# The two ends of a one-core decoder step: first transfers on two queues, products of zeros ahead of the first real ones, and a last tile added in halves

## The chip, the core and the metric

The kernel runs on one core of one Trainium2 chip. The metric is the device time of one execution in microseconds. Three runs of the kernel before took 982.81, 983.32 and 984.39 us; 983.32 is their median. The trace and the page of the profile come from one further execution, which took 982.86 us, with a span of 981.1 us from its first instruction to its last.

The engines are named as the profile names them: PE is TensorE's products and PEld its weight loads, DVE is VectorE, ACT is ScalarE, POOL is GpSimd, SP is SyncE, which issues transfers (SPq is its queue of instructions).

## What is computed

One layer of a hybrid decoder on 512 prompt positions and 8 x 4 new tokens, 544 rows of 2048 numbers in all, in float32:

```python
def rms_norm(x, g):
    xf = x.astype(jnp.float32)
    y = xf * lax.rsqrt(jnp.mean(xf * xf, axis=-1, keepdims=True) + EPS)
    return (y * g.astype(jnp.float32)).astype(x.dtype)

def project(x, g, w_in):
    z = jnp.einsum('bsd,de->bse', rms_norm(x, g), w_in)   # 2048 -> 6144: q, k, v, ga, u, gp
    ...

def merge(x, attn_o, ga, pool_o, gp, w_out):
    mix = jnp.concatenate([attn_o.reshape(b, s, ATTN_WIDTH) * jax.nn.silu(ga),
                           pool_o * jax.nn.silu(gp)], axis=-1)
    return x + jnp.einsum('bse,ed->bsd', mix, w_out)
...
y_prompt = rms_norm(hp, final_norm_g)
y_sample = rms_norm(hs, final_norm_g)
```

Between the two projections stand a windowed attention (16 heads, three dilations), for the new tokens against a cache of 2048 positions, and a pooling over 2 to 16 positions. The caches are also written out again, shifted by the new tokens. Only the input projection's first products and the last norm matter here.

## The kernel before

**Three products for one.** Every float32 operand of a large product is split into a high part, rounded to the fast float32r form, and the low rest: ScalarE makes the high part (`xH`, `wH`), VectorE subtracts it from the whole and keeps the rest (`xL`, `wL`). TensorE then adds up xH·wH, xL·wH and xH·wL in a PSUM bank.

**Order.** All instructions are written out by hand, engine by engine; nothing reorders them afterwards. A model of the engines' times inside the program (`Clock`, `Paced`) decides while the program is written out at which place of TensorE's stream the attention's pieces go. Each engine works through its list in order, and stands still where an operand isn't there. All transfers are issued by SP, in order; an issue waits where the eighth transfer before it hasn't landed, or where its buffer is in use.

**The first stage.** x comes in transposed, as 16 tiles of 128 x 544 (`x_load(d)`, 272 KB each). The first two blocks of 128 output columns (a q and a k block) are made together, tile by tile of x: for each d there are 12 products of 272 columns (two blocks, three parts, two halves of the 544 rows). Their weights come in tiles of 128 x 1024; tiles 0 and 2 are loaded and split in halves (`w_part`, `w_split`). For each d the loop calls `x_split(d)`: ScalarE makes xH (times the norm's gain, a column of the constants `c[:, C_G:]`) and the square of x, VectorE makes xL; VectorE also adds up the squares (`x_sum`). The norm's factor is applied to the finished block.

`PA` is a tile of zeros that GpSimd clears at the start; `qms` are two operands of the attention that are set to zero from it.

**The tail.** The output projection runs over four blocks of 512 columns. In each, 16 tiles e of the inner dimension are multiplied into five accumulators, four of 128 prompt rows (t = 0 to 3) and one of the new tokens (t = 4). In the last block the products of e = 10 to 15 are put off, so that the tiles finish one after the other: for each t there are 18 products of 512 columns, then an add of the input rows (`add_rows`, VectorE), the sum of squares (`squares_of`, ScalarE), the norm (`norm_of`: a sum on VectorE, the power on GpSimd), the gain (`weigh`, VectorE) and `finish`: the scaling of the whole row of 2048, split between VectorE and ScalarE, and the transfers out, 1 MB for each tile.

Of the kernel before, what the change touches and what calls it, by code (L numbers as in the profile page):

```python
# [9 lines left out]
F32 = mybir.dt.float32  # L10
F32R = mybir.dt.float32r
AF = mybir.ActivationFunctionType
ALU = mybir.AluOpType
AX = mybir.AxisListType
# [21 lines left out]
KV_LAG = 2.0  # L36
BULK_START = 22.0
BANK = 0.15

C_ID = 0  # L40
C_NBP = 128
# [171 lines left out]
def kernel(ctx: ExitStack, tc: tile.TileContext, xT, xtok, ck, cv, stT, w_in, w_pool, w_out,  # L213
                           cst, fg, y, kpT, vpT, ppT, ks, vs, psT):
    nc = tc.nc
    clock = Clock()
    pe = Paced("PE", nc.tensor, clock, _pe_cost)
    act = Paced("ACT", nc.scalar, clock, _act_cost)
    dve = Paced("DVE", nc.vector, clock, _dve_cost)
    pool = Paced("POOL", nc.gpsimd, clock, _pool_cost)  # L220
    dma = PacedDma(clock)
# [9 lines left out]
    px = clock.pool(ctx.enter_context(tc.tile_pool(name="px", bufs=2, space=PSUM)), 2)  # L231
# [86 lines left out]
    src = []  # L318
# [14 lines left out]
            if n not in (0, 2):  # L333
                dma.start(nc.sync, raw[n], src[n])

    def w_part(n, k):
        h = slice(GS // 2 * k, GS // 2 * (k + 1))
        dma.start(nc.sync, raw[n][:, h], src[n][:, h])

    def w_split(n, halves=(0, 1)):  # L340
        gh = GS // 2
# [18 lines left out]
    def w_cols(parts, lo, n):  # L360
        k, lo = divmod(lo, GS // 2)
        return parts[k][:, lo:lo + n]
# [10 lines left out]
    def x_load(d):  # L373
        if d < len(early):
            xr[d] = at.tile([128, NT], F32, name="xr", tag=early[d], bufs=limit[early[d]])
        elif d == len(early):
            xr[d] = per.tile([128, NS, 256], F32, name="kvx", tag="mixP01").rearrange("p a b -> p (a b)")[:, :NT]
        else:
            xr[d] = sa.tile([128, NS, 256], F32, name="kv", bufs=KV_BUFS).rearrange("p a b -> p (a b)")[:, :NT]
        dma.start(nc.sync, xr[d], xT[:, d, :])  # L380
# [12 lines left out]
    def x_sum():  # L393
        while squares:
            k, sq = squares.pop(0)
            dve.tensor_tensor(sums[k], sums[k], sq, ALU.add)
# [57 lines left out]
    qd = {}  # L454

    qms = [sa.tile([128, 256], F32R, name=f"qm{k}", bufs=1) for k in range(2)]
    for t in qms:
        act.activation(t, PA[:, :256], AF.Copy)

    def quad(Q):  # L460
        if Q not in qd:
# [628 lines left out]
    fillers.append([0.0, sample_all()])  # L1090
    w_load(0)
    w_load(2)
    w_part(0, 0)
    dma.start(nc.sync, c[:, C_G:], cst[:, C_G:])
    x_load(0)
    w_part(2, 0)
    x_load(1)
    x_load(2)
    w_part(0, 1)
    w_part(2, 1)  # L1100
    for d in range(3, 8):
        x_load(d)
        if d == 5:
            w_load(1)
# [29 lines left out]
    def between():  # L1134
        tick()
        if pe.t > BULK_START and dma.t < pe.t + BULK_LEAD:
            bulk_some()
# [3 lines left out]
    for d in range(DT):  # L1141
        g, r = divmod(d, spg)
        x_sum()
        x_split(d)
        if d == 0:
            w_split(2, (0,))
        elif d == 2:
            w_split(0, (1,))
            w_split(2, (1,))
            w_load(3)  # L1150
            for k in range(8, DT):
                x_load(k)
            dma.start(nc.sync, c[:, :C_G], cst[:, :C_G])
            w_load(4)
        elif d == 6:
            w_split(1)
        elif d == 7:
            w_split(3)
            w_load(5)
        elif d in (10, 12, 13):  # L1160
            w_load((6, 7, 8)[(10, 12, 13).index(d)])
        elif d == DT - 1:
            w_split(4)
            steady.append(1)
        product(ps0, g, r, d)
        product(ps1, 2 + g, r, d)
        between()
    x_sum()
    spawn(rstd_rows())
    spawn(ev_q(0, ps0), 0.4)  # L1170
# [32 lines left out]
    rows = [128, 128, 128, 128, 32]  # L1203
    fgb, xs = [None] * 4, [None] * 4
    late_loads = [(xt[t], xtok[128 * t:128 * t + 128]) for t in range(4)]
    ss = fo.tile([128, 5, 4], F32, name="ss")
    rf = fo.tile([128, 5, 2], F32, name="rf")
    for k in range(2, LATE_LEAD):
        w_load(n_in + k)
# [2 lines left out]
    for cc in range(4):  # L1212
        acc5 = [acc_tile() for _ in range(5)]
        cols = slice(512 * cc, 512 * cc + 512)

        def products(e, t):
            n, r = divmod(n_in * epg + cc * 16 + e, epg)
            for m, (a, b) in enumerate(((mixH[e], wH), (mixH[e], wL), (mixL[e], wH))):
                pe.matmul(acc5[t], a[:, 128 * t:128 * t + 128], w_cols(b[n], 512 * r, 512), start=(e == 0 and m == 0),
                          stop=(e == 15 and m == 2))  # L1220

        def sample_products(e):
            for j in range(4):
                n, r = divmod(n_in * epg + cc * 16 + e - 3 + j, epg)
                pe.matmul(acc5[4][32 * j:32 * j + 32], mixS[:, e - 3 + j], raw[n][:, 512 * r:512 * r + 512],
                          start=(e == 3), stop=(e == 15), skip_group_check=True, tile_position=(0, 32 * j))

        def part(t):
            return xt[t][:, cols] if t < 4 else xs[cc][:32]

        def add_rows(t):
            if t < 4:
                dve.tensor_tensor(part(t), acc5[t], part(t), ALU.add)
            else:
                for j in range(4):
                    dve.tensor_tensor(part(4), acc5[4][32 * j:32 * j + 32], part(4), ALU.add)

        def squares_of(t):
            nr = rows[t]
            junk = fo.tile([128, 512], F32, name="junk")  # L1240
            act.activation(junk[:nr], part(t), AF.Square, accum_out=ss[:nr, t, cc:cc + 1])

        def weigh(t):
            dve.tensor_tensor(part(t), part(t), fgb[cc][:rows[t]], ALU.mult)

        def norm_of(t):
            nr = rows[t]
            r = rf[:nr, t]
            dve.tensor_reduce(r[:, 0:1], ss[:nr, t], AX.X, ALU.add)
            pow_rstd(r[:, 1:2], r[:, 0:1], nr)  # L1250

        def finish(t):
            if t == 4:
                for j in range(4):
                    dve.tensor_scalar(xs[j][:32], xs[j][:32], rf[:32, 4, 1:2], None, op0=ALU.mult)
                    dma.start(nc.sync, y[512:544, 512 * j:512 * j + 512], xs[j][:32])
                return
            h = D * 5 // 8
            for lo, hi in ((0, h),) if t < 3 else ((0, 512), (512, h)):
                dve.tensor_scalar(xt[t][:, lo:hi], xt[t][:, lo:hi], rf[:, t, 1:2], None, op0=ALU.mult)  # L1260
                dma.start(nc.sync, y[128 * t:128 * t + 128, lo:hi], xt[t][:, lo:hi])
            act.activation(xt[t][:, h:], xt[t][:, h:], AF.Copy, scale=rf[:, t, 1:2])
            dma.start(nc.sync, y[128 * t:128 * t + 128, h:], xt[t][:, h:])

        for e in range(16):
            n, r = divmod(n_in * epg + cc * 16 + e, epg)
            if cc == 0 and r == 0:
                for k in range(e + 2, min(e + 4, 16)):
                    mix_split(k, k)
            if r == 0:  # L1270
                w_load(n + LATE_LEAD)
                w_split(n + 1)
            if cc == 0:
                if e < 4:
                    dma.start(nc.sync, *late_loads[e])
                elif e < 12:
                    j = (e - 4) % 4
                    m = per.tile([128, 512], F32, name=f"fin{e}", tag=f"mixA{e - 4}")
                    if e < 8:
                        fgb[j] = m  # L1280
                        dma.start(nc.sync, m, bass.AP(tensor=fg.tensor, offset=fg.offset + 512 * j, ap=[[0, 128], [1, 512]]))
                    else:
                        xs[j] = m
                        dma.start(nc.sync, m[:32], xtok[512:544, 512 * j:512 * j + 512])
            if (cc * 16 + e) * left // 52 < left and e:
                bulk_some((cc * 16 + e) * left // 52 - (cc * 16 + e - 1) * left // 52)
            if cc == 3 and e >= 10:
                w_split(n + 2)
                continue
            for t in range(4):  # L1290
                products(e, t)
            if e % 4 == 3:
                sample_products(e)
            if r == 1 and e < 15:
                w_split(n + 2)
        if cc < 3:
            for t in range(5):
                add_rows(t)
            w_split(n + 2)
            for t in range(5):  # L1300
                squares_of(t)
                weigh(t)
        else:
            bulk_some(len(bulk))
            sample_products(11)
            sample_products(15)
            for t in (4, 0, 1, 2, 3):
                if t < 4:
                    for e in range(10, 16):
                        products(e, t)  # L1310
                add_rows(t)
                squares_of(t)
                norm_of(t)
                weigh(t)
                finish(t)


def _constants():
# [73 lines left out]
```

## Time and profile before

| | before |
|---|---|
| median of three runs | 983.32 us (982.81 to 984.39) |
| the profiled execution | 982.86 us |
| its span | 981.1 us |
| TensorE busy | 943.6 us, 96% of the span |
| VectorE busy | 679.5 us, 69% |
| ScalarE busy | 317.0 us, 32% |
| transfers | 283.5 MB, 289 GB/s in the mean |

The span runs from the first instruction to the last; 1.76 us of the execution's time lie outside of it. All times in the rows are microseconds from the start of the span. A busy share is a mean over stages with different limits, so the rows further below are taken stretch by stretch.

### The profile page before, as it was taken

The page shows a single profiled execution, that of the slowest core. Times are in us where ns is not written, and L with a number is a line of the kernel's source. Part 1 is how long each engine was busy: PE and PEld are TensorE (multiplying, and loading weights), DVE is VectorE, ACT ScalarE, POOL GpSimd, SP SyncE. Part 2 cuts the span into 40 slices and gives each one's busy share as a digit, 9 for nine tenths or more (in the row PEclk, how much of TensorE's full clock was granted, in tenths as well). Part 3 has the DMA queues.
Part 4 walks back from the last instruction along what each step waited for, and adds up shares of the span by engine and source line. Part 5 has one row for each costly group of instructions (what it writes and reads, how often), then busy time and mean ns, then how long its engine had stood idle before and what let it go on. Part 6 is the DMA issues. An engine that isn't in the chain of part 4 may idle for free.

```text
span 981.1 us, 17768 instructions
## 1 busy us (share of the span) xinstructions
PE 943.6 (96%) x7097; PEld 841.5 (86%) x7097; DVE 679.5 (69%) x1362; ACT 317.0 (32%) x595; POOL 7.5 (1%) x20
## 2 busy tenths in 40 slices
PE   7999999999999899999999999999999999999995
PEld 7999989998888899898897899889999977777764
DVE  7654889898887798989877889753638635151524
ACT  8343332333332333422432322231222433131313
POOL 0000000000000000000000000000000000000002
PEclk9999999999999999999999999999999999999998
DMA  9989797788789789899977689899897899999954
GB/s 339 268 275 354 259 337 267 262 301 270 242 265 297 254 272 274 287 255 256 337 204 253 205 212 338 220 271 324 294 355 255 340 402 387 365 369 372 361 179 182
DMA packets 98978, 283.52 MB, mean 289 GB/s; under 512 B 12880, under 2 KB 71504, under 8 KB 94800
## 3 DMA queue, kind: packets, MB, share of 16 engines
q1 hardware_dynamic: 98896, 282.39, 86.4%
q8 instruction: 56, 0.92, 0.4%
q14 instruction: 26, 0.21, 0.1%
HBM read 271.84 MB, written 143.42 MB: 423 GB/s over the span
## 4 chain that ended last, share of the span: by engine, by line
PE 45%; DVE 5%; DMA 3%; ACT 1%; issue 1%; POOL 1%; SPq 0%; DVEq 0%; POOLq 0%; ACTq 0%
PE mm L149 30%; PE aux L149 8%; PE OS L149 4%; PE O L149 4%; DMA hist<-in_stT_dram 2%; DVE tmp L149 1%; DMA kv<-kvnew 1%; DVE SC L149 1%; DVE wL L149 1%; ACT wH L149 1%; DVE xt L149 1%; POOL rf L149 1%; SPq L174 0%; DVE P L149 0%; ACT junk L149 0%
## 5 line engine op out<-in xcount | busy, mean ns | idle before, releaser
L149 PE MATMUL mm<-xH,wH 128*128 128x272 f32 x1472 | 321.1, 299 | 6.7 <-ACT xH L149 6.5
L149 PE MATMUL mm<-xH,wL 128*128 128x272 f32 x1472 | 305.2, 289 | 0.0
L149 PE MATMUL mm<-xL,wH 128*128 128x272 f32 x1472 | 304.9, 289 | 0.0
L149 DVE TENSOR_TENSOR wL<-raw,wH 128x1024 fp32r<-128x1024 f32 (+1 forms) x128 | 154.1, 1207 | 200.5 <-ACT wH L149 200.0
L149 PEld LDWEIGHTS mm<-xH,wH 128*128 128x128 f32 x1472 | 230.4, 190 | 19.9 <-issue 12.0
L149 ACT ACTIVATE wH<-raw 128x1024 fp32r<-128x1024 f32 (+1 forms) x128 | 133.5, 1045 | 319.5 <-PE mm L149 168.2
L149 PEld LDWEIGHTS mm<-xL,wH 128*128 128x128 f32 x1472 | 232.0, 189 | 0.3 <-DVE xL L149 0.3
L149 PEld LDWEIGHTS mm<-xH,wL 128*128 128x128 f32 x1472 | 231.2, 189 | 0.0
L149 DVE TENSOR_REDUCE SC<-tmp 96x8 f32<-96x512 f32 (+2 forms) x192 | 126.2, 677 | 0.3
L149 DVE TENSOR_TENSOR tmp<-kv,aux 100x512 f32<-100x512 f32 (+2 forms) x168 | 111.6, 680 | 7.7 <-PE aux L149 6.3
L149 ACT ACTIVATE P<-P,n 128x128 f32<-128x128 f32 (+3 forms) x64 | 35.7, 558 | 94.4 <-DVE n L149 94.4
L149 ACT ACTIVATE PT<-aux 128x128 f32<-128x128 f32 (+3 forms) x64 | 27.6, 431 | 47.1 <-PE aux L149 46.7
L149 PE MATMUL aux<-cst,P 128*128 128x128 f32 x160 | 29.6, 283 | 12.0 <-DVE n L149 9.5
L149 DVE CUSTOM_DVE_ANT_0 P<-aux,cst 128x128 f32<-128x128 f32 (+3 forms) x64 | 31.0, 484 | 11.5 <-PE aux L149 11.1
L149 PE MATMUL mm<-wH,xH 128*128 128x512 f32 x96 | 38.7, 403 | 0.0
L149 PE MATMUL mm<-wH,xL 128*128 128x512 f32 x96 | 37.9, 394 | 0.0
L149 PE MATMUL mm<-wL,xH 128*128 128x512 f32 x96 | 37.8, 394 | 0.0
L149 PE MATMUL aux<-qm,oh 128*128 128x256 f32 x128 | 29.0, 308 | 6.5 <-DVE tmp L149 5.2
L149 PEld LDWEIGHTS aux<-cst,P 128*128 128x128 f32 x160 | 18.5, 140 | 17.9 <-DVE n L149 12.4
L149 PEld LDWEIGHTS aux<-qm,oh 128*128 128x128 f32 x128 | 19.5, 188 | 15.5 <-DVE tmp L149 5.3
L149 PE MATMUL aux<-wH,xH 128*128 128x512 f32 x80 | 31.9, 399 | 0.0
L149 PE MATMUL aux<-wH,xL 128*128 128x512 f32 x80 | 31.6, 395 | 0.0
(175 smaller groups left out, 1076.0 us busy)
## 6 DMA issues: line engine op xcount, KB each, us to landing
out_ks_dram<-in_ck_dram SPq DMA_DIRECT2D x112, 584.0 KB
out_vs_dram<-in_cv_dram SPq DMA_DIRECT2D x112, 584.0 KB
raw<-in_w_in_dram SPq DMA_DIRECT2D x94, 512.0 KB
kv<-in_cv_dram SPq DMA_DIRECT2D x58, 384.0 KB
kv<-in_ck_dram SPq DMA_DIRECT2D x56, 384.0 KB
raw<-in_w_out_dram SPq DMA_DIRECT2D x32, 512.0 KB
xt<-in_xtok_dram SPq DMA_DIRECT2D x4, 1024.0 KB
kv<-in_ck_dram SPq DMA_DIRECT2D x7, 512.0 KB
```

The lines of the kernel that those rows point to most:

```text
L149: return f(*args, **kw)
```

## The change

Five edits. (1) x0 heads SP's queue; the first half of weight tile 0, which headed it, is issued by ScalarE as its first instruction; the constants' column block goes behind x0. (2) 11 products of zeros, 128 x 128 x 128 in plain float32, stand ahead of TensorE's first real product; their result isn't read. (3) The two copies of zeros into `qms` move on ScalarE from the front to behind the first stage. (4) In the last block `finish` of a tile comes behind the add and the square of the next tile. (5) The products of the last tile (t = 3) are made in two halves of 256 columns, each with its own add and square; the sum of squares of that tile has five parts in place of four, and its last piece of output is issued by ScalarE.

```diff
+WARM = 11
...
-    def w_part(n, k):
+    def w_part(n, k, eng=nc.sync):
         h = slice(GS // 2 * k, GS // 2 * (k + 1))
-        dma.start(nc.sync, raw[n][:, h], src[n][:, h])
+        dma.start(eng, raw[n][:, h], src[n][:, h])
...
     qms = [sa.tile([128, 256], F32R, name=f"qm{k}", bufs=1) for k in range(2)]
-    for t in qms:
-        act.activation(t, PA[:, :256], AF.Copy)
...
-    w_part(0, 0)
+    w_part(0, 0, nc.scalar)
+    x_load(0)
     dma.start(nc.sync, c[:, C_G:], cst[:, C_G:])
-    x_load(0)
     w_part(2, 0)
     x_load(1)
     x_load(2)
     w_part(0, 1)
     w_part(2, 1)
+
+    warm = px.tile([128, 512], F32, name="aux", bufs=2)
+    for k in range(WARM):
+        pe.matmul(warm[:, :128], PA[:, :128], PA[:, :128], start=True, stop=True)
...
+    for t in qms:
+        act.activation(t, PA[:, :256], AF.Copy)
     x_sum()
     spawn(rstd_rows())
...
-        def products(e, t):
+        def products(e, t, lo=0, nr=512):
             n, r = divmod(n_in * epg + cc * 16 + e, epg)
             for m, (a, b) in enumerate(((mixH[e], wH), (mixH[e], wL), (mixL[e], wH))):
-                pe.matmul(acc5[t], a[:, 128 * t:128 * t + 128], w_cols(b[n], 512 * r, 512), start=(e == 0 and m == 0),
-                          stop=(e == 15 and m == 2))
+                pe.matmul(acc5[t][:, lo:lo + nr], a[:, 128 * t:128 * t + 128], w_cols(b[n], 512 * r, 512)[:, lo:lo + nr],
+                          start=(e == 0 and m == 0), stop=(e == 15 and m == 2), skip_group_check=(t == 3))
...
+        def last_half(k):
+            h = slice(256 * k, 256 * k + 256)
+            dve.tensor_tensor(part(3)[:, h], acc5[3][:, h], part(3)[:, h], ALU.add)
+            junk = fo.tile([128, 512], F32, name="junk")
+            act.activation(junk[:, h], part(3)[:, h], AF.Square, accum_out=ss[:, 3, 3 + k:4 + k])
...
-            dma.start(nc.sync, y[128 * t:128 * t + 128, h:], xt[t][:, h:])
+            dma.start(nc.sync if t < 3 else nc.scalar, y[128 * t:128 * t + 128, h:], xt[t][:, h:])
...
+            before = None
             for t in (4, 0, 1, 2, 3):
-                if t < 4:
+                if t < 3:
                     for e in range(10, 16):
                         products(e, t)
-                add_rows(t)
-                squares_of(t)
+                if t < 3 or t == 4:
+                    add_rows(t)
+                    squares_of(t)
+                else:
+                    for k in range(2):
+                        for e in range(10, 16):
+                            products(e, t, 256 * k, 256)
+                        last_half(k)
+                if before is not None:
+                    finish(before)
                 norm_of(t)
                 weigh(t)
-                finish(t)
+                before = t
+            finish(3)
```

The program's own model of times moves with these edits, but the attention's pieces keep their places: outside of the two ends each engine has the same instructions in the same order as before.

At the start of the program, SP's queue before (`raw` are the weight tiles, `xr` the tiles of x, `cst` the constants):

```order
L174 DMA raw<-in_w_in_dram 128x512
L174 DMA cst<-in_cst_dram 128x24
L174 DMA xr<-in_xT_dram 128x544
L174 DMA raw<-in_w_in_dram 128x512
L174 DMA xr<-in_xT_dram 128x544 x2
L174 DMA raw<-in_w_in_dram 128x512 x2
```

and now:

```order
L175 DMA xr<-in_xT_dram 128x544
L175 DMA cst<-in_cst_dram 128x24
L175 DMA raw<-in_w_in_dram 128x512
L175 DMA xr<-in_xT_dram 128x544 x2
L175 DMA raw<-in_w_in_dram 128x512 x2
```

The first transfer of weights has left this queue, and x0 stands at its head. The transfer of weights stands at the head of ScalarE's list now, which began with its table load and the two copies of zeros:

```order
L175 DMA raw<-in_w_in_dram 128x512
L150 ACT_TABLE_LOAD
L150 ACTIVATE wH<-raw 128x512
L150 ACTIVATE xH_79<-xr,cst 128x544
L150 ACTIVATE acc<-xr 128x544
L150 ACTIVATE wH<-raw 128x512
```

The split of the first weights is thereby ScalarE's first computation. At the end of the program, VectorE's list before, from the add of tile 2 on (`xt_9632` is the row tile t = 2, `xt_9633` is t = 3, `rf` the norm's factors):

```order
L149 TENSOR_TENSOR xt_9632<-OS,xt_9632 128x512
L149 TENSOR_REDUCE rf<-ss 128x1
L149 TENSOR_TENSOR xt_9632<-xt_9632,fin_9809 128x512
L149 TENSOR_SCALAR xt_9632<-xt_9632,rf 128x1280
L149 TENSOR_TENSOR xt_9633<-aux,xt_9633 128x512
L149 TENSOR_REDUCE rf<-ss 128x1
L149 TENSOR_TENSOR xt_9633<-xt_9633,fin_9809 128x512
L149 TENSOR_SCALAR xt_9633<-xt_9633,rf 128x512
L149 TENSOR_SCALAR xt_9633<-xt_9633,rf 128x768
```

and now (`xt_9643` to `xt_9645` are t = 1 to 3):

```order
L150 TENSOR_TENSOR xt_9644<-OS,xt_9644 128x512
L150 TENSOR_SCALAR xt_9643<-xt_9643,rf 128x1280
L150 TENSOR_REDUCE rf<-ss 128x1
L150 TENSOR_TENSOR xt_9644<-xt_9644,fin_9821 128x512
L150 TENSOR_TENSOR xt_9645<-aux,xt_9645 128x256 x2
L150 TENSOR_SCALAR xt_9644<-xt_9644,rf 128x1280
L150 TENSOR_REDUCE rf<-ss 128x1
L150 TENSOR_TENSOR xt_9645<-xt_9645,fin_9821 128x512
L150 TENSOR_SCALAR xt_9645<-xt_9645,rf 128x512
L150 TENSOR_SCALAR xt_9645<-xt_9645,rf 128x768
```

Each scaling (`TENSOR_SCALAR`) has moved behind the add of the tile after it, and the last add has become two of 256 columns.

## Rows read from the trace of the kernel before

**Rows 1.** The page: busy time, share of the span, instructions of each engine.

```profile
PE 943.6 (96%) x7097; PEld 841.5 (86%) x7097; DVE 679.5 (69%) x1362; ACT 317.0 (32%) x595; POOL 7.5 (1%) x20
```

**Rows 2.** Busy time by stretch, the start: length, engines, granted clock, transfer share, GB/s.

```profile
core 0: us, PE busy (x) PEld busy (x) DVE busy (x) ACT busy (x) POOL busy (x), PEclk, DMA share, GB/s
...
1.50:3.53 2.03, 0.00 (x0) 0.00 (x0) 0.00 (x0) 1.22 (x4) 0.00 (x0) 1.00 0.78 185
3.53:5.69 2.16, 0.00 (x0) 0.00 (x0) 0.69 (x1) 0.63 (x1) 0.00 (x0) 1.00 0.86 244
...
6.50:12.25 5.75, 5.75 (x24) 5.43 (x25) 4.79 (x7) 5.75 (x11) 0.00 (x0) 1.00 1.02 376
12.25:21.40 9.15, 9.15 (x73) 9.15 (x73) 9.15 (x16) 9.15 (x17) 0.00 (x0) 1.00 1.04 412
21.40:34.10 12.70, 12.44 (x99) 12.22 (x98) 12.70 (x19) 9.01 (x14) 0.00 (x0) 1.00 0.97 318
```

**Rows 3.** Timeline around d = 8: start, duration, engine, operation, [idle before, releaser].

```profile
21.39 0.78 DVE L149 SCALAR_TENSOR_TENSOR xL<-xr,cst,xH 128x544 fp32r<-128x544 f32 x1
...
22.22 0.52 PE L149 MATMUL mm<-xL,w 128*128 128x272 f32 x2 [0.26 <-DVE xL L149]
...
22.72 0.78 DVE L149 SCALAR_TENSOR_TENSOR xL<-xr,cst,xH 128x544 fp32r<-128x544 f32 x1
```

**Rows 4.** Timeline of the first 8 us, SP's issues and ScalarE.

```profile
0.72 0.39 SPq L174 DMA_DIRECT2D raw<-in_w_in_dram  x1
...
2.01 0.72 ACT L149 ACTIVATE qm<-PA 128x256 fp32r<-128x256 f32 x2
...
3.53 0.63 ACT L149 ACTIVATE wH<-raw 128x512 fp32r<-128x512 f32 x1 [0.80 <-DMA raw<-in_w_in_dram]
...
5.69 0.75 ACT L149 ACTIVATE xH<-xr,cst 128x544 fp32r<-128x544 f32 x1 [1.54 <-DMA xr<-in_xT_dram]
...
7.44 0.75 ACT L149 ACTIVATE xH<-xr,cst 128x544 fp32r<-128x544 f32 x1
```

**Rows 5.** Timeline of the tail: the last tile's products and its way to the scaling.

```profile
966.23 0.40 PE L149 MATMUL aux<-wH,xH 128*128 128x512 f32 x1
...
970.18 0.40 PE L149 MATMUL aux<-wH,xL 128*128 128x512 f32 x1
...
971.56 0.89 DVE L149 TENSOR_SCALAR xt<-xt,rf 128x1280 f32<-128x1280 f32 x1 [0.70 <-POOL rf L149]
...
972.36 0.68 DVE L149 TENSOR_TENSOR xt<-aux,xt 128x512 f32<-128x512 f32 x1
...
973.14 0.63 ACT L149 ACTIVATE junk<-xt 128x512 f32<-128x512 f32 x1 [0.64 <-DVE xt L149]
...
973.89 0.16 DVE L149 TENSOR_REDUCE rf<-ss 128x1 f32<-128x4 f32 x1 [0.85 <-ACT junk L149]
...
975.36 1.02 DVE L149 TENSOR_SCALAR xt<-xt,rf 128x512 f32<-128x512 f32 x2 [0.71 <-POOL rf L149]
```

**Rows 6.** Busy time by stretch, the tail; columns as in the second group.

```profile
973.25:976.00 2.75, 0.00 (x0) 0.00 (x0) 1.40 (x4) 1.25 (x3) 1.10 (x2) 0.84 0.95 381
976.00:976.50 0.50, 0.00 (x0) 0.00 (x0) 0.38 (x1) 0.29 (x1) 0.00 (x0) 0.50 0.00 0
976.50:979.50 3.00, 0.00 (x0) 0.00 (x0) 0.00 (x0) 0.00 (x0) 0.00 (x0) 0.50 0.91 350
979.50:981.10 1.60, 0.00 (x0) 0.00 (x0) 0.00 (x0) 0.00 (x0) 0.00 (x0) 0.50 0.00 0
```

**Rows 7.** Groups by shape: busy us, mean ns of one, idle before.

```profile
L149 DVE TENSOR_TENSOR zr<-mm,rstd 128x272 f32<-128x272 f32 x30 | 11.7, 432 | 0.0
...
L149 PE MATMUL aux<-kHH,qS 128*128 128x256 f32 x16 | 4.5, 281 | 0.0
...
L149 PEld LDWEIGHTS mm<-xH,wL 128*128 128x128 f32 x1472 | 231.2, 189 | 0.0
```

**Rows 8.** Timeline: products in plain float32 at the fast pace.

```profile
35.67 2.06 PE L149 MATMUL aux<-ones,acc 128*128 128x1 f32 x20
```

More of the change, by code (lines that the diff above doesn't have):

```diff
@@ L1205 @@
     late_loads = [(xt[t], xtok[128 * t:128 * t + 128]) for t in range(4)]
-    ss = fo.tile([128, 5, 4], F32, name="ss")
+    ss = fo.tile([128, 5, 5], F32, name="ss")
     rf = fo.tile([128, 5, 2], F32, name="rf")
@@ L1248, in norm_of @@
             r = rf[:nr, t]
-            dve.tensor_reduce(r[:, 0:1], ss[:nr, t], AX.X, ALU.add)
+            dve.tensor_reduce(r[:, 0:1], ss[:nr, t, :5 if t == 3 else 4], AX.X, ALU.add)
             pow_rstd(r[:, 1:2], r[:, 0:1], nr)
```

## The prediction

> **What bounds the kernel now.** I read the page's busy shares first: TensorE is busy for 96% of the span, VectorE for 69% [rows 1], so time can be won only where TensorE stands still or runs slowly, or after its last product. The change touches two such places, the first 34 us and the last 12 us, so I read busy time by stretch next.
>
> The start [rows 2]. TensorE does nothing before 6.5 us. From 6.50 to 12.25 it does 24 products in 5.75 us, 0.24 us each; from 12.25 to 21.40, 73 of the same form in 9.15 us, 0.125 us each. The clock column reads 1.00 in both, but by the pace the first stretch ran at the lower of the two levels. VectorE matters more here: it is busy for all of 12.25 to 21.40 and of 21.40 to 34.10. It makes the xL tiles that TensorE needs. The timeline of the hand-over shows it [rows 3]: xL of d = 8 is begun at 21.39 and takes 0.78 us, and TensorE, after 0.26 us of standing still, takes it up at 22.22. So, slow pace and all, TensorE reached d = 8 ahead of its operand. From there it is the slower one (0.125 us x 12 = 1.5 us per d; an xL is begun every 1.33 us, 21.39 to 22.72). The first stage therefore ends a fixed time after xL of d = 8, and that hangs on the chain of splits, not on TensorE's clock.
>
> What the chain hangs on is in the timeline of its first steps [rows 4]. ScalarE splits the first weights at 3.53, then stands still for 1.54 us until x0 lands (5.69); from there it goes from operation to operation without a gap, and VectorE follows it with gaps under 0.5 us until it has none.
>
> The tail [rows 5]. TensorE's last product starts at 970.18 and takes 0.40 us, but VectorE adds tile 3 only at 972.36, 1.8 us later: it waited at 971.56 for the norm of tile 2 and scaled that first. Then square (973.14), sum (973.89), the power on GpSimd, and the scaling at 975.36. After it only transfers [rows 6]: tile 2's 1 MB flows from 973.25 to 976.0, tile 3's from 976.5 to 979.5, 1.6 us of closing follow.
>
> **The change, part by part.** On the engines between the two places the same instructions stand in the same order, so what the start gains or loses should be carried to the tail as a shift.
>
> *Tail, order.* The add of tile 3 no longer stands behind the scaling of tile 2, so it can follow TensorE. The last tile's 18 products of 512 columns, 0.232 us apart (966.23 to 970.18 is 17 steps, [rows 5]), become 36 of 256. The trace has no row of that shape in such a sequence; the nearest is the 272-column product with a weight load of its own, 0.125 us [rows 2]. By columns alone it would be 0.118. The last product then starts at 966.23 + 35 x 0.118 to 0.125 = 970.36 to 970.60, as against 970.18; with 0.28 us to its end (a 256-column product, [rows 7]) and about 0.1 for the hand-over (0.05 in [rows 3]) the second half-add starts at 970.75 to 971.0. A VectorE operation on 272 columns out of PSUM takes 0.43 us [rows 7], so it ends near 971.3 and tile 2's scaling starts there, some 0.3 us earlier than now (971.56). ScalarE's second square has half the columns: from 0.75 us between its start and the sum (973.14 to 973.89, [rows 5]) at most half of the square's 0.63 goes, I take 0.2, so the sum could start near 972.0; it waits for tile 2's scaling (0.89 us) until 972.15. From sum to scaling took 973.89 to 975.36 = 1.47 us, so tile 3 is scaled at about 973.6, 1.75 us earlier than now.
>
> But the transfers take most of that away again. Tile 2's data started 1.7 us after its scaling (971.56 to 973.25, [rows 5, 6]), so now near 973.0, and needs 2.75 us: to 975.75. Tile 3's data could start 1.1 us after its scaling (975.36 to 976.5), at 974.75, but the engines are full for another microsecond; at tile 2's rate the two MB flow from 973.0 to 978.4 or 978.5. The last byte was at 979.5. **Tail: 1.1 us gained.** Bounds: 1.75 if the transfers don't queue; at the other end see the rival on weight loads. Issuing the last piece from ScalarE spares SP one issue of about 0.4 us (as at the start, [rows 4]), which lies under the queued data: nothing. If the queue were empty it would be worth up to that.
>
> *Start, transfers.* x0 now heads SP's queue and the first weights go out of ScalarE's. By bytes: the first weights, the small constants and x0 are 540 KiB = 553 KB; 185 GB/s over 1.50 to 3.53 moved 376 KB, and the rest at 244 GB/s takes 0.73 us [rows 2]: both in by 4.26. ScalarE's split of the weights (0.63) and of x0 (0.75) then come one behind the other, and xH0 starts at 4.8 to 4.9 where it started at 5.69. The next link is x1: ScalarE went from xH0 to xH1 in 1.75 us (5.69 to 7.44, [rows 4]), and x1 must be there. By bytes the first five big pieces (1094 KB) are in by 6.35; in the trace x1 was taken at 7.44 without a wait, so it may have landed at any time up to that. Hence the chain moves up by at most 7.44 - 6.35 = 1.1 us. If x0 comes no sooner than now (5.69) and the weights beside it, the split of the weights no longer lies in the wait, and the chain is up to 0.63 us later. I take the middle of what bytes and chain allow: **start 0.5 us gained**, between -0.6 and +1.1.
>
> *Start, products of zeros.* 11 products of 128 x 128 in plain float32, ahead of the first real one, once GpSimd has cleared their operand. The nearest row is that of the sums of squares: 10 float32 products (20 records) in 2.06 us at the fast pace [rows 8], 0.21 us each, 0.41 at the slow one, so 11 take 2.3 to 4.5 us and end before 6 us. They stand in front of products that can start at 5.6 at best. Even if they ended 2 us later nothing would be lost: TensorE needs 8 x 1.5 = 12 us at the fast pace ahead of 21.4. What they give back is the slow stretch, and by [rows 3] TensorE only waits longer for xL: **0 us**. Cover: VectorE's chain; without it the 24 products would be worth 5.75 - 24 x 0.125 = 2.75 us.
>
> *The copies of zeros moved behind the first stage* take 0.72 us of ScalarE [rows 4]. Before, they lay in the wait for the weights; now they stand ahead of a weight split at about 29 us, where ScalarE is busy for 9.0 of 12.7 us and VectorE for all of it [rows 2], so that split waits in VectorE's queue anyhow: nothing.
>
> Sum: 1.1 + 0.5 = 1.6 us. The profiled execution took 982.86 (a span of 981.1 and 1.8 around it, which stays), so 981.26; the median of the three runs shown is 0.46 above it, which makes 981.7 in its terms, 0.16% less.
>
> **The rivals.**
> *Transfers share the engines.* The Trainium skill (DMA: Bandwidth & Descriptors, "Issuing engines are not separate DMA queues") says that transfers issued from several engines interleave on the same 16 DMA engines and that a second issuer saves only issue time. By that, x0 and the weights land together and late. Worked out from rows without it: if x0's landing stays, the start gives between 0 and -0.6, in sum 0.5 to 1.1 gained, 982.2 to 982.8. For it: the engines are 86% busy from 3.53 to 5.69 [rows 2]. Against it: by bytes x0 was 1.4 us late. Chance 0.12.
>
> *The clock was the bound.* If TensorE's own pace sets the end of the first stage, 2.75 us come back on top of the tail, 3.9 in sum: 979.5. Against it stands the wait in [rows 3]. Here the page TensorE: Matmul & The Clock Gate (Part 1) of the Trainium skill bears: the array's clock is low by default and activity releases it; the pace in [rows 2] agrees, and no run here shows yet that products of zeros count as activity. Chance 0.06.
>
> *The tail isn't held by transfers and the start pays in full:* 1.75 + 0.5 to 1.1, 980.5 to 981.1. Chance 0.16.
>
> *Weight loads pace the half-width products (slower).* Each is charged a weight load of 0.19 us [rows 7]; if that is the step, 36 take 6.8 us where 4.2 stood, the second half-add comes at 973.2, and tile 2, whose scaling now stands behind it, at 973.6: both tiles flow from 975.3 to 980.8, 1.3 us later than now. 984.6 without the start, 984.1 with it. The point at which it eats the tail's gain is a step of about 0.15 us. Against it: the 272-column row has the same load hidden in 0.125. Chance 0.04.
>
> *The middle answers to the shift.* A moved start meets other transfers; nothing but the 1.6 us between the three runs prices it. A loss of 2 us or more: 0.06.
>
> **How the numbers follow.** My forecast (both parts pay, 0.8 to 2.3 us) holds 0.56, and 981.7 is its middle. About 0.2%, 2 us, is what a measurement of this kernel can tell from no change: 0.20 of the forecast, the third and the second rival lie beyond it, 0.42 faster; 0.36 of the forecast, the first rival and most of the fourth make 0.51 the same; 0.07 is slower. Leaving out the clock and the worst of the middle, the range is 980.2 to 983.9; the forecast alone has 981.0 to 982.5.
>
> **What would show it.** Right: xH0 before 5.2 us, TensorE at the fast pace from its first real product but standing still for two to three microseconds in all before d = 8, xL of d = 8 about 0.5 us earlier; the last add within 0.4 us of the last product; tile 2's and tile 3's data without a gap between them. Wrong: no such waits while the stage ends 2 us or more earlier (clock), xH0 at 5.7 or later (shared engines), half-width products more than 0.15 us apart, or a gap in the data at the end.

## The result and the profile after

| | before | after |
|---|---|---|
| median (lowest to highest) | 983.65 us (982.81 to 984.39) | 1000.43 us (999.80 to 1000.53) |
| the profiled execution, its span | 982.86, 981.1 us | 1000.53, 998.7 us |

The changed kernel is slower: the ratio is 1.017 [1.0152, 1.0187]. The forecast was 981.7 us in a range of 980.2 to 983.9, so it was wrong, and none of its rivals named what happened. In the experiments further below, two executions far above all others of their kernels (1151 and 2096 us) stand in the medians, but not in the ratios. The first line of the page answers to [rows 1]:

```profile
PE 946.7 (95%) x7137; PEld 845.0 (85%) x7137; DVE 679.1 (68%) x1363; ACT 316.8 (32%) x597; POOL 7.6 (1%) x20
```

TensorE has 40 more records than before: 22 for the products of zeros, 18 for those that were cut in halves. Otherwise no engine has more than 0.1 us of work more. The span grew by 17.6 us all the same, so something waits. Busy time by stretch shows where (length, then the engines, granted clock, share of the transfer engines, GB/s); the first three rows answer to [rows 2], the others show the end:

```profile
6.50:12.25 5.75, 5.33 (x38) 4.92 (x38) 4.79 (x8) 5.75 (x12) 0.00 (x0) 1.00 0.99 358
12.25:21.40 9.15, 8.10 (x62) 7.62 (x60) 9.15 (x15) 9.15 (x17) 0.00 (x0) 1.00 1.04 409
21.40:34.10 12.70, 11.93 (x95) 11.79 (x94) 12.70 (x19) 9.70 (x17) 0.00 (x0) 1.00 0.98 322
...
930.00:954.00 24.00, 24.00 (x115) 17.26 (x117) 6.26 (x6) 3.65 (x5) 0.00 (x0) 1.00 0.49 168
954.00:971.00 17.00, 16.39 (x89) 12.61 (x81) 12.53 (x23) 5.25 (x12) 4.11 (x8) 1.00 0.00 1
971.00:981.00 10.00, 2.35 (x18) 2.15 (x18) 2.90 (x6) 2.77 (x6) 1.35 (x3) 0.75 0.23 77
981.00:990.00 9.00, 0.00 (x0) 0.00 (x0) 0.00 (x0) 0.00 (x0) 0.00 (x0) 0.50 0.85 316
```

The kernel before has this row for the fifth of them:

```profile
954.00:971.00 17.00, 16.57 (x72) 13.08 (x70) 11.22 (x22) 4.77 (x10) 3.81 (x8) 1.00 0.31 116
```

From 954 to 971 nothing moves now (1 GB/s in place of 116), though the new tokens' rows and tiles 0 and 1 are scaled by then. From 981 on no engine computes, and the data flows, at 316 GB/s up to 990. Work that should have lain under TensorE's products has been pushed behind them. SP's row in the timeline names the place (start, duration of the issue):

```profile
933.34 0.51 SPq L175 DMA_DIRECT2D out_vs_dram<-in_cv_dram  x1
935.41 0.51 SPq L175 DMA_DIRECT2D out_ks_dram<-in_ck_dram  x1
979.42 0.51 SPq L175 DMA_DIRECT2D out_vs_dram<-in_cv_dram  x1
979.98 0.59 SPq L175 DMA_DIRECT2D out_ks_dram<-in_ck_dram  x1
980.61 0.59 SPq L175 DMA_DIRECT2D out_vs_dram<-in_cv_dram  x1
981.30 1.95 SPq L175 DMA_DIRECT2D out_y_dram<-fin  x4
983.34 9.29 SPq L175 DMA_DIRECT2D out_y_dram<-xt  x8
```

The waits of SP's queue from 940 us on (what was waited for: us in total, times, longest) say for what:

```profile
SPq L175 <- DMA out_y_dram<-xt: 43.5, 1, 43.5
```

SP stood 43.5 us in front of a copy of the cache, a transfer that needs no computed operand, until an *output* transfer had landed. The only output that was under way by then is the last piece of the last tile, which ScalarE had issued:

```profile
975.99 0.94 ACT L150 ACTIVATE xt<-xt,rf 128x768 f32<-128x768 f32 x1 [0.74 <-POOL rf L150]
976.95 0.35 ACTq L175 DMA_DIRECT2D out_y_dram<-xt  x1
```

Why a copy of the cache waits for that transfer, the order of instructions with their waits tells. The program gives each transfer one of eight semaphores (DMAHW0 to 7) in turn, and an issue waits for the transfer that last used its semaphore. SP's list, by row number:

```
630 L175 DMA out_ks_dram<-in_ck_dram 16x9344 [waits DMAHW0_49]
631 L175 DMA out_vs_dram<-in_cv_dram 16x9344 [waits DMAHW1_49]
632 L175 DMA out_ks_dram<-in_ck_dram 16x9344 [waits DMAHW3_49]
...
638 L175 DMA out_ks_dram<-in_ck_dram 16x9344 [waits DMAHW1_49]
639 L175 DMA out_vs_dram<-in_cv_dram 16x9344 [waits DMAHW2_49]
```

and ScalarE's last transfer:

```
476 L175 DMA out_y_dram<-xt_9645 128x768 [waits DMAHW2_49,Activation_49]
```

Between SP's rows 631 and 632 the semaphore DMAHW2 is skipped: ScalarE's last output got that turn, ahead of SP's last 22 transfers. Eight turns on, row 639 has DMAHW2 again and must wait until the kernel's last scaling is done and its output has landed. Row 639 is the copy at 979.42; it, two more copies and all other outputs had to wait. By size they are 3 x 584 KB, 4 x 64 KB and 4 MB less ScalarE's piece of 384 KB, 5.86 MB in all, and 17.7 us at the 330 GB/s that the view by stretch gives for 979.4 to 997.1 move 5.84 MB.

### The profile page after: what moved, and what is told of

It reads as the page before. It is cut to its first block, busy times and chain, and to the rows that moved or that the text cites. A ratio compares the mean times of both kernels' runs of the same rounds, so it can differ in the third digit from the quotient of the medians.

```text
span 998.7 us, 17850 instructions
## 1 busy us (share of the span) xinstructions
PE 946.7 (95%) x7137; PEld 845.0 (85%) x7137; DVE 679.1 (68%) x1363; ACT 316.8 (32%) x597; POOL 7.6 (1%) x20
## 4 chain that ended last, share of the span: by engine, by line
PE 47%; DVE 4%; DMA 2%; ACT 1%; issue 1%; SPq 0%; DVEq 0%; POOLq 0%; POOL 0%; ACTq 0%
PE mm L150 30%; PE aux L150 8%; PE OS L150 4%; PE O L150 4%; DMA hist<-in_stT_dram 2%; DVE tmp L150 1%; ACT wH L150 1%; DVE wL L150 1%; DVE SC L150 1%; SPq L175 0%; DVE xt L150 0%; DVE P L150 0%; DVE mixS L150 0%; DVE zr L150 0%; ACT PT L150 0%
## 5 line engine op out<-in xcount | busy, mean ns | idle before, releaser
L150 PE MATMUL aux<-wH,xH 128*128 128x512 f32 (+1 forms) x86 | 33.1, 384 | 0.6 <-DVE xt L150 0.6
L150 PE MATMUL aux<-wH,xL 128*128 128x512 f32 (+1 forms) x86 | 32.5, 378 | 0.0
```

The lines of the kernel that those rows point to most:

```text
L150: return f(*args, **kw)
```

## The experiments

The kernels were timed in two jobs: the last piece back on SP, the last piece on ScalarE alone, the tail's edits alone and the start's edits alone in the first, the other four in the second. The kernel before had medians of 984.24 us (29 runs) and 984.97 us (29 runs) there. Each ratio is against the runs of its own job.

**The last piece back on SP.** All of the change but the issuer of the last piece:

```diff
-            dma.start(nc.sync if t < 3 else nc.scalar, y[128 * t:128 * t + 128, h:], xt[t][:, h:])
+            dma.start(nc.sync, y[128 * t:128 * t + 128, h:], xt[t][:, h:])
```

> The changed kernel with one edit undone: SP issues the last piece of output again. Theory A (the turn): transfers of both issuers take turns on eight semaphores, ScalarE's last transfer got a turn ahead of SP's last ones, and SP stands before a cache copy until that output has landed. Then SP never stands for tens of us, the cache copies are out before the tail, and 16 to 18 us come back: 982.4 to 984.3. Theory B (the new order of adds and scalings, or the halves, hold the outputs back): the time stays near 1000.

Measured: 984.02 us, ratio 1.0001 [0.999, 1.0011]. The semaphores go around without a gap, and SP issues its copies to the end in good time:

```profile
934.97 0.51 SPq L175 DMA_DIRECT2D out_vs_dram<-in_cv_dram  x1
936.71 0.51 SPq L175 DMA_DIRECT2D out_ks_dram<-in_ck_dram  x1
938.36 0.51 SPq L175 DMA_DIRECT2D out_vs_dram<-in_cv_dram  x1
963.33 1.76 SPq L175 DMA_DIRECT2D out_y_dram<-fin  x4
967.35 12.66 SPq L175 DMA_DIRECT2D out_y_dram<-xt  x9
```

The whole loss hangs on who issues this one transfer; the new order and the halves don't cause it.

**The last piece on ScalarE alone.** The kernel before with only that edit, the reverse of the diff above:

> The kernel before with one edit of the change alone: ScalarE issues the last piece of output. Theory A: SP stops before a cache copy at about 935 us and goes on when that piece has landed, 2.5 us after its issue at 976.3, so at about 979; three cache copies and all other outputs then take as long as in the changed kernel (17.7 us), closing 1.6: a span of 998, a time of 999 to 1000. Theory B: no more than 0.5 us from the kernel before, 983 to 984.

Measured: 1003.23 us, ratio 1.0192 [1.0178, 1.0206]. SP's waits and the two issues around the longest one:

```profile
SPq L174 <- DMA out_y_dram<-xt: 46.2, 1, 46.2
```

```profile
935.61 0.51 SPq L174 DMA_DIRECT2D out_ks_dram<-in_ck_dram  x1
982.29 0.51 SPq L174 DMA_DIRECT2D out_vs_dram<-in_cv_dram  x1
```

The edit alone is enough. It costs 19 us here and 16.4 in the changed kernel (1000.43 less the 984.02 above), because the wait hangs on the last scaling, which comes 2.83 us later here (978.82 and 975.99 on ScalarE). Of this 1.2 us are the old order (the scaling stands 9.14 us behind tile 3's first product in place of 7.92); the other 1.6 us are a later start of tile 3 in this trace (969.68 and 968.07).

**A dose: ScalarE issues a piece of tile 0 instead.** That piece is ready some 10 us earlier, so by the theory SP must go on that much earlier.

```diff
-            dma.start(nc.sync if t < 3 else nc.scalar, y[128 * t:128 * t + 128, h:], xt[t][:, h:])
+            dma.start(nc.scalar if t == 0 else nc.sync, y[128 * t:128 * t + 128, h:], xt[t][:, h:])
```

> The changed kernel with ScalarE issuing a piece of tile 0 in place of tile 3's last. Theory A: SP stops at the same kind of place (a cache copy that shares the turn) and goes on when that piece has landed, about 2.5 us after its issue at 966.5, so at 969 in place of 979; three or four cache copies (2 MB) and all outputs but that piece (3.8 MB) need 15 us from there, partly held up by their own scalings: a span of 985 to 988, a time of 987 to 990, a dozen below the changed kernel. Rival, any transfer issued by ScalarE in the tail costs the same: 1000.

Measured: 991.56 us, ratio 1.007 [1.0051, 1.0088], a little above the expected 987 to 990, and far from the 1000 of the rival. SP's and ScalarE's issues:

```profile
933.55 0.51 SPq L175 DMA_DIRECT2D out_vs_dram<-in_cv_dram  x1
...
968.87 0.51 SPq L175 DMA_DIRECT2D out_ks_dram<-in_ck_dram  x1
```

```profile
966.38 0.36 ACTq L175 DMA_DIRECT2D out_y_dram<-xt  x1
```

SP is released 2.49 us after ScalarE's issue (in the changed kernel 979.42 - 976.95 = 2.47). The turn skipped in SP's list is now DMAHW1, between rows 630 and 631, and the row that stands is 638, with DMAHW1. SP goes on 10.55 us earlier than in the changed kernel and the time is 8.9 us shorter; as the turn is one earlier, four copies in place of three stand behind it, some 1.8 us of transfer at 330 GB/s. The wait follows ScalarE's transfer.

**The tail's edits alone,** with the last piece on SP and the start of before:

```diff
...
+                else:
+                    for k in range(2):
+                        for e in range(10, 16):
+                            products(e, t, 256 * k, 256)
+                        last_half(k)
+                if before is not None:
+                    finish(before)
...
```

> The kernel before with the tail's edits alone (adds ahead of scalings, last tile in halves), last piece on SP. Theory A and the trace of the changed kernel (the second half waits 0.6 us for the first half-add, so the last product starts at 966.2 + 5.0 = 971.2): tile 2 is scaled at about 971.9, both tiles flow from 973.6 to 979.1 in place of 979.5, 0.4 us gained, 983.2. My first sum had 1.1 gained, 982.5. Theory B: near 1000.

Measured: 984.08 us, ratio 0.9999 [0.9987, 1.0011]. In the trace the tail, from tile 3's first product to the end of the span, takes 14.52 us (967.98 to 982.5), as against 14.87 before (966.23 in [rows 5] to 981.1): 0.35 us gained, which the timed runs can't show.

**The last tile whole.** To see what the halves do, the additions stay ahead of the scalings, and tile 3 is made in one piece (start of before). Against the kernel above:

```diff
-                if t < 3:
+                if t < 4:
                     for e in range(10, 16):
                         products(e, t)
-                if t < 3 or t == 4:
-                    add_rows(t)
-                    squares_of(t)
-                else:
-                    for k in range(2):
-                        for e in range(10, 16):
-                            products(e, t, 256 * k, 256)
-                        last_half(k)
+                add_rows(t)
+                squares_of(t)
...
```

> The kernel before with the adds ahead of the scalings, but the last tile whole, and all outputs on SP. Counted from the first product of tile 3 to the end of the span (14.87 us in the trace of before, 14.52 in the tail alone with halves). If the halves cost what they save because the second half waits for the first half-add (0.6 us) and the adds are two: the last product ends 4.35 us after the first, the add starts 0.1 later, tile 2 is scaled 5.15 us after the first product, both tiles flow from 6.9 to 12.3, so 13.9. Rival, the halves are worth having: 14.6 or more.

Measured: 984.0 us, ratio 0.9993 [0.9979, 1.0008]. The tail's rows:

```profile
968.43 0.40 PE L150 MATMUL aux<-wH,xH 128*128 128x512 f32 x1
...
972.38 0.40 PE L150 MATMUL aux<-wH,xL 128*128 128x512 f32 x1
...
972.81 0.69 DVE L150 TENSOR_TENSOR xt<-aux,xt 128x512 f32<-128x512 f32 x1 [1.89 <-PE aux L150]
...
973.42 0.88 DVE L150 TENSOR_SCALAR xt<-xt,rf 128x1280 f32<-128x1280 f32 x1
...
975.82 1.02 DVE L150 TENSOR_SCALAR xt<-xt,rf 128x512 f32<-128x512 f32 x2 [0.71 <-POOL rf L150]
```

The tail takes 13.87 us (968.43 to 982.3), 0.65 less than in halves.

**Tile 2 scaled ahead of the last add.** As the kernel above, but for the last tile the scaling stands first again; tiles 4 to 1 keep the new order:

```diff
+                if t == 3:
+                    finish(before)
                 add_rows(t)
                 squares_of(t)
-                if before is not None:
+                if before is not None and t < 3:
                     finish(before)
```

> As the one before, but tile 2 is scaled ahead of the last add: its factors are ready 3.4 us after tile 3's first product, the last product ends at 4.35. If the queue of transfers sets the end: tile 2 flows from 5.1 to 7.8, tile 3 is scaled at 7.4 and flows from 8.6 to 11.5, closing 1.6: 13.1, 1.8 us shorter than before. Rival, the chain behind the last add sets the end and the order of scalings is all one: 13.9 as in the one before.

Measured: 983.86 us, ratio 0.9991 [0.9978, 1.0005]; the tail 13.11 us (969.19 to 982.3), the shortest of all:

```profile
969.19 0.40 PE L150 MATMUL aux<-wH,xH 128*128 128x512 f32 x1
...
972.40 0.89 DVE L150 TENSOR_SCALAR xt<-xt,rf 128x1280 f32<-128x1280 f32 x1 [0.71 <-POOL rf L150]
...
973.58 0.69 DVE L150 TENSOR_TENSOR xt<-aux,xt 128x512 f32<-128x512 f32 x1 [0.29 <-PE aux L150]
...
976.58 1.02 DVE L150 TENSOR_SCALAR xt<-xt,rf 128x512 f32<-128x512 f32 x2 [0.71 <-POOL rf L150]
```

In its trace the tail is 1.8 us shorter than before, but tile 3 starts 2.96 us later (969.19 and 966.23), so the span is no shorter, and the interval of the timed runs holds 1: it is not shown to be faster.

**The start's edits alone:** zeros, two queues and the moved copies, on the kernel before.

```diff
...
-    w_part(0, 0)
+    w_part(0, 0, nc.scalar)
+    x_load(0)
     dma.start(nc.sync, c[:, C_G:], cst[:, C_G:])
-    x_load(0)
...
```

> The kernel before with the start's edits alone (x0 first, first weights from ScalarE, products of zeros, copies of zeros later). By the trace of the changed kernel xL of d = 8 starts at 21.47 in place of 21.39, so 0.1 us later: 983.7, no change. If the loss of 1.8 us that the changed kernel shows at 640 us comes from the moved start, this one has it too: 985.5. If it is chance, it hasn't, or not in most runs.

Measured: 985.69 us, ratio 1.0018 [1.0007, 1.003]. No gain, and a small loss whose interval lies clear of 1. With the 0.6 us by which the kernel before is slower in this job (984.24 and 983.65), the two expected times become 984.3 and 986.1; the measured one lies nearer the second, and its trace has the wait near 640 us that is shown at "The middle" below.

**No products of zeros.** The kernel with the last piece on SP, without them:

```diff
-WARM = 11
+WARM = 0
```

> The changed kernel with the last piece on SP and without the products of zeros. If VectorE's chain sets the end of the first stage: TensorE runs at the slow pace for some 5.7 us from its first product at 6.6, reaches d = 8 within 0.5 us of its operand, and the time is that of the kernel with the zeros to 0.5 us, 984.0. Rival, the clock was the bound: 2.7 us slower, 986.7.

Measured: 984.49 us, ratio 0.9997 [0.9982, 1.0012]. The start by stretch and in the timeline:

```profile
6.50:12.25 5.75, 5.36 (x27) 5.04 (x28) 4.79 (x8) 5.75 (x11) 0.00 (x0) 1.00 1.03 370
```

```profile
6.89 0.82 PE L150 MATMUL mm<-xH,wH 128*128 128x272 f32 x2 [6.89 <-ACT xH L150]
...
22.58 0.52 PE L150 MATMUL mm<-xL,w 128*128 128x272 f32 x2 [0.76 <-DVE xL L150]
```

Without zeros the first stretch has 27 products, with them 38, and yet TensorE still arrives at d = 8 ahead of xL, by 0.76 us where up to 0.5 was expected. The zeros buy standing time, and nothing that the time shows.

## Why the prediction was wrong, and where it was right

**The step that failed** is "Issuing the last piece from ScalarE spares SP one issue of about 0.4 us (as at the start, [rows 4]), which lies under the queued data: nothing." It looked at what the moved transfer costs, and not at what the move does to the transfers left on SP. The kernel was known to make an issue wait for the eighth transfer before it. While one engine issues everything, that transfer is always an older one of the same list. With a second issuer it is the eighth by the program's count, and there ScalarE's last output stands ahead of SP's last 22 transfers, ten of them cache copies that need no computed operand. The term is not 0 but +16 us (in the changed kernel) to +19 us (alone). The three kernels that move this piece show it: back on SP the time is 984.02, alone on ScalarE it gives 1003.23, and with a piece of tile 0 in its place 991.56. "On the engines between the two places the same instructions stand in the same order" was true, and hid it: the same rows had other waits. Why the program counts that transfer so early stays open; it doesn't go by the time at which a piece is ready, since tile 0's piece, issued 10.57 us earlier, got a turn only one earlier.

**The tail, order and queue: right.** The last add follows TensorE (in the tail alone 0.32 us behind the start of the last product, 973.29 and 972.97), and the two tiles' data run one behind the other: from 975.0 to 978.0 at 354 GB/s, from 978.0 to 981.0 at 345, and every half microsecond in between carries data, where 976.0 to 976.5 stood empty before [rows 6]. The tails can be laid side by side, in us after tile 3's first product:

| | tile 2 scaled | tile 3 scaled | end |
|---|---|---|---|
| before | 5.33 | 9.13 | 14.87 |
| tail alone (halves) | 5.65 | 7.90 | 14.52 |
| last tile whole | 4.99 | 7.39 | 13.87 |
| tile 2 ahead of the add | 3.21 | 7.39 | 13.11 |

Two rules fit all four rows: the end comes 5.7 us after tile 3's scaling (before, and the last row: 5.74 and 5.72) or 8.9 us after tile 2's (8.87 and 8.88 in the middle rows), whichever is later. Three kernels that were not used for the rules bear them out: 8.90 and 8.91 us behind tile 2's scaling with the last piece back on SP and without zeros, 5.68 behind tile 3's with the start alone. With the new order tile 2's data, not tile 3's scaling, holds the end. The last two rows show it most plainly: tile 3 is scaled at the same 7.39, tile 2 1.78 us earlier, and the end comes 0.76 earlier.

**The tail, size: 1.1 us forecast, 0.35 found.** The pace of the half-width products was right, (970.07 - 968.07) / 17 = 0.118 us, and the rival on weight loads falls. The mis-sized term is "the second half-add starts at 970.75 to 971.0". The timeline of the changed kernel answers to [rows 5]:

```profile
968.07 0.28 PE L150 MATMUL aux<-wH,xH 128*128 128x256 f32 x1
...
970.07 0.27 PE L150 MATMUL aux<-wH,xL 128*128 128x256 f32 x1
...
970.48 0.42 DVE L150 TENSOR_TENSOR xt<-aux,xt 128x256 f32<-128x256 f32 x1
...
970.95 0.38 PE L150 MATMUL aux<-wH,xH 128*128 128x256 f32 x1 [0.61 <-DVE xt L150]
...
973.39 0.42 DVE L150 TENSOR_TENSOR xt<-aux,xt 128x256 f32<-128x256 f32 x1 [2.49 <-PE aux L150]
973.73 0.88 DVE L150 TENSOR_SCALAR xt<-xt,rf 128x1280 f32<-128x1280 f32 x1
```

The second half doesn't follow at 970.19: it starts at 970.95, when VectorE has read the first half out of the same accumulator. So the second half-add comes 5.32 us behind tile 3's first product (973.39 - 968.07), where 4.5 to 4.8 was forecast. That puts tile 2's scaling 5.66 us behind the first product where 5.07 was forecast (971.3 - 966.23), and tile 2's scaling sets the end. The halves cost more than they gain: whole, the tail is 0.65 us shorter.

**The start: 0.5 us forecast, none found.** The first rival was right there.

```profile
1.30 5.06 PE L150 MATMUL aux<-PA 128*128 128x128 f32 x22 [1.30 <-POOL PA L150]
...
5.30 0.63 ACT L150 ACTIVATE wH<-raw 128x512 fp32r<-128x512 f32 x1 [2.86 <-DMA raw<-in_w_in_dram]
...
5.83 0.73 ACT L150 ACTIVATE xH<-xr,cst 128x544 fp32r<-128x544 f32 x1
...
6.62 0.52 PE L150 MATMUL mm<-xH,wH 128*128 128x272 f32 x2 [0.26 <-ACT xH L150]
...
21.47 0.78 DVE L150 SCALAR_TENSOR_TENSOR xL<-xr,cst,xH 128x544 fp32r<-128x544 f32 x1
...
22.31 0.52 PE L150 MATMUL mm<-xL,w 128*128 128x272 f32 x2 [0.77 <-DVE xL L150]
```

The weights' split waits until 5.30 where it began at 3.53, and xH0 starts at 5.83 where it was 5.69 [rows 4]. In the other kernels with these edits it starts at 5.54 to 6.11, in those without at 5.26 to 5.50. The first weights came later with two issuers: their split starts at 5.00 to 5.57 in the five kernels with these edits, at 3.53 to 3.77 in the five without. x0's split follows it without a wait, so when x0 landed the trace doesn't show; its split comes no earlier. The step that failed here is "both in by 4.26", which gave the first 553 KB to these pieces alone. In the changed kernel 175 GB/s over 1.50 to 3.53 and 301 over 3.53 to 5.30 make 0.89 MB by the time at which the weights' split could begin: later pieces shared the engines with the first ones. The prediction took it as a sign against its first rival that x0 was 1.4 us behind its bytes in the kernel before; 0.90 MB had moved there by 5.69 [rows 2], so it was a sign for it. The Trainium skill says (DMA: Bandwidth & Descriptors, "Issuing engines are not separate DMA queues") that transfers interleave on the same DMA engines whichever engine issued them, and that a second issuer saves only issue time. The bytes of the changed kernel agree with the first, and nothing in the start's rows speaks against the second. xL of d = 8 begins at 21.47 (21.39 in [rows 3]); over all kernels it is 21.18 to 21.74 with the edits and 21.39 to 22.09 without, so the first stage ends about when it did.

**The zeros: 0, right.** They took 5.06 us (2.3 to 4.5 forecast) and ended at 6.36, not before 6; the first real product, which waited for xH0, came at 6.62. Behind them TensorE goes at the fast pace: two products take 0.52 us, as at 22.31, where the first two without zeros took 0.82 (and so they did in one of the four kernels with zeros), and 6.50 to 12.25 has 38 products where 24 stood [rows 2]. The granted-clock column reads 1.00 in either, so here the number of products tells the level. The Trainium skill has it (TensorE: Matmul & The Clock Gate, Part 1) that activity releases the clock, and these rows show that products of zeros count as such. TensorE waits 2.1 us for xL from 6.5 up to and with d = 8, as against 0.3 before: the forecast said two to three. The rival that the clock was the bound falls, by this and by the run without zeros.

**The middle** is not shown to be a cost of the change. TensorE starts tile 3 at 968.07, 1.84 us later than before, and most of it is one wait near 640 us, behind the output of an attention step:

```profile
PE aux L150 <- ACT ov L150: 2.1, 1, 2.1
```

It is 0.4 us in the trace of before, 1.3, 0.4 and none in three kernels with the start of before and other tails, 2.2 in the kernel before with only the last piece moved, and 0.6, 2.2, 2.4 or none in those with the new start. It comes and goes with either start, one trace each. What decides it stays open, and so does the 0.18% by which the start alone is slower, since the kernel with the last piece on SP has the same start and shows no loss.

## What to carry to other kernels

Before a transfer is moved to another engine, look at the waits of the transfers that stay: where all share semaphores in turn, a late transfer on one engine can hold an early one on the other, and everything queued behind it. A comparison of the order alone doesn't show this; one with the waits does, a skipped semaphore in the list. When a tail is bound by its data, the tile to hurry is the one whose transfer starts first, not the last one computed.

## What the hardware showed that was not expected

A plain float32 product of 128 x 128 x 128 took 0.37 to 0.46 us at the start (11 took 4.08, 4.91, 5.06 and 5.06 us in four kernels), where a one-column one at the fast pace took 0.21 us [rows 8]. From the issue of a 384 KB output on idle transfer engines to the release of the issue that waited for it 2.47 to 2.50 us passed in three kernels. And halves of one accumulator are not free to overlap in this program: TensorE's first product into the second half waited 0.61 us for VectorE's read of the first (0.56 to 0.62 in the four other kernels with halves).
